# A two-layer trunk in split float32: weight low parts behind the gating, gate's first products ahead of up's, sums between the last transposes, and some pair sums in two DMAs

## The chip, the cores and the metric

The kernel runs on 1 core of one Trainium2 chip. The metric is device time in microseconds of one execution; the time before is the median of 3 runs. Engines are named as the profile names them: PE (matmuls, with PEld for its weight loads), DVE, ACT, POOL and SP; SP issues most DMAs, POOL those that add in flight, ACT a few.

## The reference, cut to what matters

16 learned tokens and 512 given ones make 528 rows of width 1024. Two layers follow, and a last RMSNorm; the learned rows are dropped at the end.

```python
for i in range(DEPTH):                       # 2
    h = h + 0.5 * swiglu(rmsnorm(h, norm_ffn1[i]), ffn1_w_in[i], ffn1_w_out[i])
    h = h + mixer_i(rmsnorm(h, norm_mix[i]))     # retention, then gated linear attention
    h = h + 0.5 * swiglu(rmsnorm(h, norm_ffn2[i]), ffn2_w_in[i], ffn2_w_out[i])
h = rmsnorm(h, final_norm)[:, N_META:]

def swiglu(x, w_in, w_out):
    gate, up = jnp.split(x @ w_in, 2, axis=-1)   # 1024 -> 2 x 2816
    return (jax.nn.silu(gate) * up) @ w_out      # 2816 -> 1024
```

All of it is float32.

## The kernel before, in words

**Layout.** The hidden width lies on the 128 partitions (8 tiles `x[d]`), tokens lie along the free axis, in two halves of 264 columns (256 in the last SwiGLU, which leaves out the learned tokens). The four SwiGLUs are called f10, f20, f11 and f21 (first or second of the layer, then the layer); each has 22 tiles of 128 hidden features for gate and 22 for up.

**Three products for one.** Each float32 operand is split in a high and a low part, `hi` (a cast, L154 for weights, L425 for values, both on ACT) and `lo` (the rest, L155 and L426, on DVE). `mm3` makes one product of three matmuls: hi x hi (L392), hi x lo of the values (L393), lo of the weights x hi (L394).

**Units of seven.** Most weight tiles are used in pairs, by a Strassen-like scheme (`unit_steps`): a unit takes a 2 x 2 block of weights (two feature tiles, two halves of the contraction) and the two token halves, and makes 7 products instead of 8, in the order `a11, s1, s2, a12, s3, s4, a22`. The parts `s1` to `s4` are sums of weight blocks. Two of these sums are made in flight: `pair[:, 0]` and `pair[:, 1]` are loaded with blocks a11 and a22 by SP (L122), and a DMA issued by POOL adds a21 to both (L123). `s1` reads `pair[:, 1]`, `s3` reads `pair[:, 0]`. The other two are made by DVE (L160, L162). Products go to one PSUM bank X and a two-bank tile QZ; ACT copies intermediate results out (L604, L606, L610) before the bank is added to again.

**Weights.** The class `Weights` holds a plan of all weight parts in the order of use. `_load` issues loads as buffers come free (7 raw, 3 pair), `_split` makes a part's `hi` and `lo` (7 buffers). `get` is called at the head of a step, `free` and `hook` (which calls `fetch`, four parts ahead) at its end.

**Order of a SwiGLU** (`ffn_steps`). The first tiles are plain (`"p"`), the others units: gate (`"i", "g"`), then up (`"i", "u"`), then, a gate unit behind the end of a group of hidden tiles, the output units (`"o"`) of that group; f21 has groups of 6, 6, 6 and 4 tiles, the others of 8, 6 and 8. So the output units of f21's first group lie between the gate unit and the up unit of tiles 6 and 7. In the last up unit of f10, f20 and f11 (`last` in `unit_u`) the hidden value is split in two parts: `row1` adds (L830), gates (L831) and calls `hidden(..., 0)`; `c21` gates the rest (L842) and calls `hidden(..., 1)`. The output units of the last group start right behind it.

**Order on the engines.** Each engine runs its instructions in an order that the tile framework lays down when the program is built, by readiness and priority; `urgent()` raises the priority, `issue_after(ins)` puts what is inside behind `ins`. A part that is issued later in the code can therefore stand earlier on an engine.

**Start.** x and the first weights (512 columns each, gate's first) are loaded by SP in turn. Nine matmuls on ones (L356) keep PE busy meanwhile. `plain_first` then makes gate and up of tile 0 together, over 8 contraction tiles k, per k: gate on both halves, then up on both halves, six matmuls each. Meanwhile ACT and DVE scale and split x (L468, L470) and sum its squares (L476 to L487), which PE then reduces (L514).

**End** (`out_last`). The last output tiles are made plainly (`pl`). For the second token half each tile's residual (L976), square (L981 on ACT, summed by DVE at L984) and gained value `xg` (L989) are made as it is finished; the last square is kept apart. Then each `xg[d]` is transposed, 128 tokens at a time (L1033, two per d), PE reduces the squares (L1040), DVE and POOL make the scale (L1045, L1047), ACT and DVE apply it (L1053, L1055), and SP writes four blocks of 128 x 512 (L1056).

Of the kernel before, what the change touches and what calls it, by code (L numbers as in the profile page):

```python
# [13 lines left out]
AF = mybir.ActivationFunctionType  # L14
# [47 lines left out]
class Weights:  # L62
# [10 lines left out]
    def __init__(self, tc, ctx, raw_bufs=7, pair_bufs=3, bufs=7):  # L73
        self.nc, self.tc = tc.nc, tc

        self.behind = None
        self.raw_pool = ctx.enter_context(tc.tile_pool(name="wraw", bufs=raw_bufs))
        self.pair_pool = ctx.enter_context(tc.tile_pool(name="wpair", bufs=pair_bufs))
        self.pool = ctx.enter_context(tc.tile_pool(name="wsplit", bufs=bufs))

        self.homes = [(self.pool, bufs, set())]
        self.ahead = AHEAD


        self.loads = {"raw": [], "pair": []}
        self.begun = dict.fromkeys(self.loads, 0)
        self.over = dict.fromkeys(self.loads, 0)
        self.room = {"raw": raw_bufs, "pair": pair_bufs}
        self.tiles, self.plan, self.parts = {}, [], {}
        self.split = self.taken = self.keys = 0  # L90
# [6 lines left out]
            self.loads["raw"].append(((c, o), len(self.plan), (part,)))  # L97
            self.plan.append((key, c, o, part.shape[1], None))

    def add_unit(self, key, ap1, ap2, order):  # L100
        c = self.keys
        self.keys += 1
        n = ap1.shape[1] // 2
        a = {"a11": ap1[:, :n], "a12": ap1[:, n:], "a21": ap2[:, :n], "a22": ap2[:, n:]}
        self.loads["pair"].append((c, len(self.plan), (a["a11"], a["a22"], a["a21"])))
        for q in ("a11", "a12", "a22"):
            self.loads["raw"].append(((c, q), len(self.plan), (a[q],)))
        for q in order:
            self.plan.append((key + (q,), c, q, n, order))

    def _load(self):
        nc = self.nc
        for kind, loads in self.loads.items():
            while self.begun[kind] < min(self.over[kind] + self.room[kind], len(loads)):
                c, first, aps = loads[self.begun[kind]]
                if kind == "pair" and first > self.split + 3 * len(self.UNIT):
                    break
                n = aps[0].shape[1]
                if kind == "pair":
                    t = self.pair_pool.tile([P, 2, PW], F32, tag="pair", name=f"pair{c}")[:, :, :n]  # L120
                    for i in range(2):
                        nc.sync.dma_start(t[:, i], aps[i])  # L122
                    nc.gpsimd.dma_start(t, aps[2].unsqueeze(1).broadcast_to([P, 2, n]), accum_op=ALU.add)  # L123
                else:
                    t = self.raw_pool.tile([P, PW], F32, tag="raw", name=f"raw{self.begun[kind]}")[:, :n]
                    nc.sync.dma_start(t, aps[0])
                self.begun[kind] += 1
                self.tiles[c] = t

    def _split(self, upto):  # L130
        V = self.nc.vector
        while self.split < min(upto, len(self.plan)):
# [17 lines left out]
            with ExitStack() as order_:  # L150
                if self.behind and i < self.FRONT:
                    for ins in self.behind:
                        order_.enter_context(self.tc.issue_after(ins.ins))
                self.nc.scalar.copy(hi[:, :n], raw)  # L154
                V.tensor_sub(lo[:, :n], raw, hi[:, :n].bitcast(F32))  # L155
            self.parts[i] = (hi, lo)
            self.split += 1
# [55 lines left out]
def trunk(ctx, tc, a):  # L213
# [30 lines left out]
    def plan_ffn(w_in, w_out, layer, which, last=False, late=False):  # L244
        first = True
        for kind, a_, b_ in ffn_steps(last, late):
            key = (which, layer, kind, a_, b_)
            o = b_ + (NF if a_ == "u" else 0)
            if kind == "p":
                if late and b_ == 0:  # L250

                    if a_ == "g":
                        for q in range(2):
                            for s in range(2):
                                W.add((which, layer, kind, "gu"[s], 0, q), w_in[layer, s * NF, :, q * PW:(q + 1) * PW])
                else:
                    W.add(key, w_in[layer, o])
            elif kind == "i":
                W.add_unit(key, w_in[layer, o], w_in[layer, o + 1], W.FIRST if first else W.UNIT)
                first = False  # L260
            else:
                f0, f1 = (LAST_GROUPS if last else GROUPS)[a_]
                c = slice(f0 * P, f1 * P)
                if kind == "o":
                    W.add_unit(key, w_out[layer, b_, :, c], w_out[layer, b_ + 1, :, c], W.UNIT)
                else:
                    W.add(key, w_out[layer, b_, :, c])

# [378 lines left out]
    def ffn(which, layer, halves, gcol, feed, late=False):  # L647
# [5 lines left out]
        with tc.tile_pool(name=f"h_{me}", bufs=4) as hp, tc.tile_pool(name=f"t_{me}", bufs=1) as tp, \  # L653
# [135 lines left out]
            def plain_first():  # L789

                ps, out = zip(*[halves_of(f"p{me}{s}0") for s in "gu"])
                for q in range(2):
                    ws = [W.get((which, layer, "p", s, 0, q)) for s in "gu"]
                    for k in range(KD // 2 * q, KD // 2 * (q + 1)):
                        for i in range(2):
                            for hf, (r0, r1) in enumerate(halves):
                                mm3(ps[i][hf], *W.at(ws[i], k % (KD // 2) * P), uh[k][:, r0:r1], ul[k][:, r0:r1],
                                    k == 0, k == KD - 1)
                    for w in ws:
                        W.free(w)  # L800
                        hook()
# [20 lines left out]
                return g  # L822

            def unit_u(f, g, first):
                y = []
                last = feed and f + 2 == NF

                def row1(ab, qz):
                    o = y[0][:, 2:]
                    V.tensor_add(o, ab, qz)  # L830
                    V.tensor_mul(o, o, pair(g[0], halves))  # L831
                    if last:
                        hidden(f, y[0], 0)

# [6 lines left out]
                def c21(c):  # L841
                    V.scalar_tensor_tensor(y[0][:, 0], c, -1.0, g[1][:, a0:a1], ALU.mult, ALU.mult)  # L842
                    if last:
                        hidden(f, y[0], 1)

                unit((which, layer, "i", "u", f), f"{me}u{f}", W.FIRST if first else W.UNIT, halves, 4, rhs_in, up_,
                     row1, c22, c21)
# [5 lines left out]
            def unit_o(gi, d, behind):  # L853
# [22 lines left out]
                        feed(d + 1, ins)  # L876

                unit((which, layer, "o", gi, d), f"{me}o{gi}{d}", W.UNIT, halves, len(hs), rhs, up_, row1, c22, c21, behind)

            first, outs, g = True, {}, []  # L880
            steps = ffn_steps(feed is None, late)
# [82 lines left out]
    def out_last(key, hh, hl, halves, scale):  # L964
# [67 lines left out]
            for j in range(2):  # L1032
                nc.tensor.transpose(yt[j][:, d // 4, (d % 4) * P:(d % 4 + 1) * P], xg[d][:, j * P:(j + 1) * P], ident)  # L1033

        for d in range(KD - 2):
            turn(d)
        st = bank("st_fb")
        for i, sq in enumerate((sqa[1], last)):
            for j in range(2):
                nc.tensor.matmul(st[:, j:j + 1], lhsT=sq[:, j * P:(j + 1) * P], rhs=ones[:, 0:1],  # L1040
                                 start=(i + j == 0), stop=(i == 1), skip_group_check=True)
        for d in range(KD - 2, KD):
            turn(d)
        ms = tmp.tile([P, 8], F32, tag="ms", name="ms_fb")
        V.tensor_scalar(ms[:, :2], st[:, :2], 1.0 / D, EPS, ALU.mult, ALU.add)  # L1045
        r = tmp.tile([P, 8], F32, tag="r", name="r_fb")
# [1 line left out]
        for b in range(2):  # L1048
            for j in range(2):
                ys = (tmp.tile([P, T], F32, tag="hf", name=f"yb{j}{b}") if j else  # L1050
                      tail_[:, 6 + b, :])[:, :512]
                if j == 0:
                    S.activation(ys, yt[j][:, b, :], AF.Copy, scale=r[:, j:j + 1])  # L1053
                else:
                    V.tensor_scalar(ys, yt[j][:, b, :], r[:, j:j + 1], None, ALU.mult)  # L1055
                nc.sync.dma_start(a["out_b"][j * P:(j + 1) * P, b * 512:(b + 1) * 512], ys)  # L1056


    def retention(feed):
# [974 lines left out]
```

## Time and profile before

| | |
|---|---|
| runs, us | 2075.05, 2076.25, 2075.76; median 2075.76 |
| profiled execution, us | 2076.74, its span 2075.0 |
| mean granted clock of PE | 0.999 |
| DVE, ACT, POOL busy | 86%, 57%, 10% of the span |
| DMA | 318.84 MB, 154 GB/s over the span |

The profile records one execution. A row of the timeline is: start, duration (both us from the span's start), engine, line, operation, output <- inputs, shapes, count, and in brackets the idle time before it with what ended it. A row of windows is: stretch, its length, then busy time and instructions of the engines asked for, the granted clock, the DMA engines' busy share and GB/s. A matmul's duration includes its way through the array; how fast PE works is read from the distance of starts.

### The profile page before, as it was taken

The numbers are of one execution on the slowest core, as the hardware profiler recorded it, in microseconds if no ns is written. First come the engines' busy times: TensorE is split into PE (matmuls) and PEld (weight loads), VectorE is DVE, ScalarE is ACT, GpSimd is POOL, SyncE is SP. The second block draws the span as 40 slices with busy tenths as digits, with TensorE's granted clock in tenths as the row PEclk, the third lists the DMA queues.
The fourth block names the chain that finished last, engine by engine and source line by source line (L and its number), as shares of the span: only waits on it lengthen the run. The fifth ranks groups of instructions, "written<-read, shape, count | busy, mean of one in ns | idle before, by whom it ended". The sixth has DMA issues, their size and how long they took to land. (4 is left out here: it accounts for less than half of the span.)

```text
span 2075.0 us, 42965 instructions
## 1 busy us (share of the span) xinstructions
PE 2062.4 (99%) x16367; PEld 2018.1 (97%) x16367; DVE 1789.7 (86%) x3214; ACT 1192.7 (57%) x2329; POOL 206.1 (10%) x175
## 2 busy tenths in 40 slices
PE   9999999999999999999999999999999999999998
PEld 9999999999999999999999999999999988999998
DVE  8988889968686879988889998889997968998886
ACT  5656566554545455656566565666645445666664
POOL 1011111010101000111111011110101000111110
PEclk9999999999999999999999999999999999999999
DMA  7676777355555532776776377677614351687772
GB/s 223 152 195 158 198 179 188 104 139 137 137 139 126 144 101 69 180 189 159 188 190 183 108 179 182 150 208 174 198 57 122 88 164 61 163 210 174 181 179 72
DMA packets 175871, 318.84 MB, mean 154 GB/s; under 512 B 17456, under 2 KB 40368, under 8 KB 175664
## 3 DMA queue, kind: packets, MB, share of 16 engines
q1 hardware_dynamic: 133856, 237.30, 34.8%
q0 software_dynamic: 40800, 75.51, 23.0%
q10 hardware_dynamic: 1008, 3.29, 0.5%
q8 instruction: 128, 2.10, 0.4%
q14 instruction: 79, 0.65, 0.1%
HBM read 311.76 MB, written 4.26 MB: 152 GB/s over the span
## 5 line engine op out<-in xcount | busy, mean ns | idle before, releaser
L154 ACT CAST whi<-raw 128x512 fp32r<-128x512 f32 (+1 forms) x893 | 526.0, 606 | 484.2 <-DVE raw L160 97.4
L155 DVE TENSOR_TENSOR wlo<-raw,whi 128x512 fp32r<-128x512 f32 (+1 forms) x893 | 584.7, 671 | 145.1 <-ACT whi L154 136.4
L154 ACT CAST whi<-pair 128x512 fp32r<-128x512 f32 (+1 forms) x304 | 183.5, 604 | 120.3 <-PE Xf11u L393 7.3
L155 DVE TENSOR_TENSOR wlo<-pair,whi 128x512 fp32r<-128x512 f32 (+1 forms) x304 | 202.5, 666 | 7.7 <-ACT whi L154 6.3
L123 POOL DMA_DIRECT2D pair<-in_f_in x75 | 91.1, 1214 | 770.5 <-DVE wlo L155 264.1
L160 DVE TENSOR_TENSOR raw<-pair,raw 128x512 f32<-128x512 f32 (+1 forms) x146 | 97.5, 668 | 2.5
L162 DVE TENSOR_TENSOR raw<-raw,raw 128x512 f32<-128x512 f32 (+1 forms) x146 | 97.4, 667 | 2.4
L123 POOL DMA_DIRECT2D pair<-in_f_out x48 | 58.1, 1210 | 413.8 <-DVE wlo L155 161.2
L393 PE MATMUL po_r<-ogl,whi 128*128 128x264 f32 x256 | 72.7, 284 | 0.0
L392 PE MATMUL po_r<-ogh,whi 128*128 128x264 f32 x256 | 72.5, 283 | 0.0
L394 PE MATMUL po_r<-ogh,wlo 128*128 128x264 f32 x256 | 72.5, 283 | 0.0
L123 POOL DMA_DIRECT2D pair<-in_ret_in x20 | 24.3, 1216 | 295.9 <-DMA pair<-in_ret_in 96.8
L392 PE MATMUL Xf20o<-hf,whi 128*128 128x264 f32 x176 | 50.9, 289 | 0.2
L392 PE MATMUL Xf11o<-hf,whi 128*128 128x264 f32 x176 | 50.9, 289 | 0.2
L392 PE MATMUL Xf10o<-hf,whi 128*128 128x264 f32 x176 | 50.8, 289 | 0.2
L393 PE MATMUL Xf10o<-hf,whi 128*128 128x264 f32 x176 | 50.0, 284 | 0.0
L393 PE MATMUL Xf11o<-hf,whi 128*128 128x264 f32 x176 | 50.0, 284 | 0.0
L393 PE MATMUL Xf20o<-hf,whi 128*128 128x264 f32 x176 | 50.0, 284 | 0.0
L394 PE MATMUL Xf11o<-hf,wlo 128*128 128x264 f32 x176 | 49.9, 285 | 0.0
L394 PE MATMUL Xf10o<-hf,wlo 128*128 128x264 f32 x176 | 49.9, 285 | 0.0
L394 PE MATMUL Xf20o<-hf,wlo 128*128 128x264 f32 x176 | 49.9, 284 | 0.0
L394 PEld LDWEIGHTS po_r<-ogh,wlo 128*128 128x128 f32 x256 | 48.2, 188 | 0.0
(985 smaller groups left out, 8519.9 us busy)
## 6 DMA issues: line engine op xcount, KB each, us to landing
raw<-in_f_in SPq DMA_DIRECT2D x277, 256.0 KB, 4.5
pair<-in_f_in SPq DMA_DIRECT2D x150, 256.0 KB, 4.7
pair<-in_f_in POOLq DMA_DIRECT2D x75, 512.0 KB, 6.6
raw<-in_f_out SPq DMA_DIRECT2D x80, 256.0 KB, 3.9
raw<-in_ret_in SPq DMA_DIRECT2D x76, 256.0 KB, 3.4
raw<-in_f_out SPq DMA_DIRECT2D x72, 192.0 KB, 3.2
pair<-in_f_out SPq DMA_DIRECT2D x48, 256.0 KB, 4.2
pair<-in_f_out POOLq DMA_DIRECT2D x24, 512.0 KB, 6.0
```

What stands on the lines that cost most here:

```text
L123: nc.gpsimd.dma_start(t, aps[2].unsqueeze(1).broadcast_to([P, 2, n]), accum_op=ALU.add)
L154: self.nc.scalar.copy(hi[:, :n], raw)
L155: V.tensor_sub(lo[:, :n], raw, hi[:, :n].bitcast(F32))
L160: V.tensor_add(s2, self.tiles[c][:, 1], self.tiles[c, "a11"])
L162: V.tensor_add(raw, raw, s2)
L392: nc.tensor.matmul(ps, lhsT=lh, rhs=rh, start=start, stop=False, **kw)
L393: nc.tensor.matmul(ps, lhsT=lh, rhs=rl, start=False, stop=False, **kw)
L394: return nc.tensor.matmul(ps, lhsT=ll, rhs=rh, start=False, stop=stop, **kw)
```

## The change

Five edits:

1. `Weights.late`: in the last up unit of f10, f20 and f11 the gating's multiplication (L831) is kept; from the end of `c21` to the end of the next output unit every low part of a weight (L155) is issued behind it.
2. `plain_first`: for k = 0, up's six products are issued behind gate's last.
3. `parted`: for the two input units of tiles 6 and 7 of f21 and the four output units of its first group, SP loads `pair[:, 1]` first, and POOL adds a21 in two DMAs, `pair[:, 1]` first, instead of one.
4. The end: the sums of squares come behind the transposes of 4 tiles instead of 6; the other 4 tiles are issued behind them.
5. The output: the first block is scaled and written in two halves of 256 columns, and the last block is written by a DMA that ACT issues.

```diff
-                    for i in range(2):
+                    for i in (1, 0) if parted[0] else (0, 1):
                         nc.sync.dma_start(t[:, i], aps[i])
-                    nc.gpsimd.dma_start(t, aps[2].unsqueeze(1).broadcast_to([P, 2, n]), accum_op=ALU.add)
+                    if parted[0]:
+                        for i in (1, 0):
+                            nc.gpsimd.dma_start(t[:, i], aps[2], accum_op=ALU.add)
+                    else:
+                        nc.gpsimd.dma_start(t, aps[2].unsqueeze(1).broadcast_to([P, 2, n]), accum_op=ALU.add)
...
                 self.nc.scalar.copy(hi[:, :n], raw)
+                if self.late:
+                    order_.enter_context(self.tc.issue_after(self.late.ins))
                 V.tensor_sub(lo[:, :n], raw, hi[:, :n].bitcast(F32))
...
-                W.add_unit(key, w_in[layer, o], w_in[layer, o + 1], W.FIRST if first else W.UNIT)
+                W.add_unit(key, w_in[layer, o], w_in[layer, o + 1], W.FIRST if first else W.UNIT,
+                           last and b_ == LAST_GROUPS[1][0])
...
-                    W.add_unit(key, w_out[layer, b_, :, c], w_out[layer, b_ + 1, :, c], W.UNIT)
+                    W.add_unit(key, w_out[layer, b_, :, c], w_out[layer, b_ + 1, :, c], W.UNIT, last and a_ == 0)
...
-                            for hf, (r0, r1) in enumerate(halves):
-                                mm3(ps[i][hf], *W.at(ws[i], k % (KD // 2) * P), uh[k][:, r0:r1], ul[k][:, r0:r1],
-                                    k == 0, k == KD - 1)
+                            with tc.issue_after(ins.ins) if k == 0 and i == 1 else ExitStack():
+                                for hf, (r0, r1) in enumerate(halves):
+                                    ins = mm3(ps[i][hf], *W.at(ws[i], k % (KD // 2) * P), uh[k][:, r0:r1],
+                                              ul[k][:, r0:r1], k == 0, k == KD - 1)
...
-                    V.tensor_mul(o, o, pair(g[0], halves))
+                    late[0] = V.tensor_mul(o, o, pair(g[0], halves))
...
                     if last:
                         hidden(f, y[0], 1)
+                        W.late = late[0]
...
                 unit((which, layer, "o", gi, d), f"{me}o{gi}{d}", W.UNIT, halves, len(hs), rhs, up_, row1, c22, c21, behind)
+                W.late = None
...
-        for d in range(KD - 2):
+        for d in range(KD - 4):
             turn(d)
...
-        for d in range(KD - 2, KD):
-            turn(d)
+        with tc.issue_after(ins.ins):
+            for d in range(KD - 4, KD):
+                turn(d)
...
-                nc.sync.dma_start(a["out_b"][j * P:(j + 1) * P, b * 512:(b + 1) * 512], ys)
+                for o in (0, 256) if b + j == 0 else (0,):
+                    c = slice(o, 256 + o if b + j == 0 else 512)
+                    if j == 0:
+                        S.activation(ys[:, c], yt[j][:, b, c], AF.Copy, scale=r[:, j:j + 1])
+                    else:
+                        V.tensor_scalar(ys[:, c], yt[j][:, b, c], r[:, j:j + 1], None, ALU.mult)
+                    (nc.scalar if b + j == 2 else nc.sync).dma_start(
+                        a["out_b"][j * P:(j + 1) * P, b * 512 + c.start:b * 512 + c.stop], ys[:, c])
```

`ins` in the end is the last of the matmuls that reduce the squares.

More of the change, by code (lines that the diff above doesn't have):

```diff
@@ L76, in __init__ @@
         self.behind = None
+        self.late = None
         self.raw_pool = ctx.enter_context(tc.tile_pool(name="wraw", bufs=raw_bufs))
@@ L98, in add, with add_unit @@
             self.plan.append((key, c, o, part.shape[1], None))
-    def add_unit(self, key, ap1, ap2, order):
+    def add_unit(self, key, ap1, ap2, order, parted=False):
         c = self.keys
@@ L104, in add_unit @@
         a = {"a11": ap1[:, :n], "a12": ap1[:, n:], "a21": ap2[:, :n], "a22": ap2[:, n:]}
-        self.loads["pair"].append((c, len(self.plan), (a["a11"], a["a22"], a["a21"])))
+        self.loads["pair"].append((c, len(self.plan), (a["a11"], a["a22"], a["a21"]), parted))
         for q in ("a11", "a12", "a22"):
@@ L114, in _load @@
             while self.begun[kind] < min(self.over[kind] + self.room[kind], len(loads)):
-                c, first, aps = loads[self.begun[kind]]
+                c, first, aps, *parted = loads[self.begun[kind]]
                 if kind == "pair" and first > self.split + 3 * len(self.UNIT):
@@ L824, in unit_u @@
             def unit_u(f, g, first):
-                y = []
+                y, late = [], [None]
                 last = feed and f + 2 == NF
@@ L1039, in out_last @@
             for j in range(2):
-                nc.tensor.matmul(st[:, j:j + 1], lhsT=sq[:, j * P:(j + 1) * P], rhs=ones[:, 0:1],
-                                 start=(i + j == 0), stop=(i == 1), skip_group_check=True)
-        for d in range(KD - 2, KD):
-            turn(d)
+                ins = nc.tensor.matmul(st[:, j:j + 1], lhsT=sq[:, j * P:(j + 1) * P], rhs=ones[:, 0:1],
+                                       start=(i + j == 0), stop=(i == 1), skip_group_check=True)
+        with tc.issue_after(ins.ins):
+            for d in range(KD - 4, KD):
+                turn(d)
         ms = tmp.tile([P, 8], F32, tag="ms", name="ms_fb")
@@ L1051, in out_last @@
                       tail_[:, 6 + b, :])[:, :512]
[L1052 to L1055, printed above, removed]
-                nc.sync.dma_start(a["out_b"][j * P:(j + 1) * P, b * 512:(b + 1) * 512], ys)
+                for o in (0, 256) if b + j == 0 else (0,):
[6 more added lines that the diff above has]
+                        a["out_b"][j * P:(j + 1) * P, b * 512 + c.start:b * 512 + c.stop], ys[:, c])
     def retention(feed):
```

## The prediction

> **What bounds the kernel now.** I read the page first, then the waits of PE, then stretches of the timeline around each of them.
>
> ```profile
> span 2075.0 us, 42965 instructions
> ...
> PE 2062.4 (99%) x16367; PEld 2018.1 (97%) x16367; DVE 1789.7 (86%) x3214; ACT 1192.7 (57%) x2329; POOL 206.1 (10%) x175
> ...
> PE pf10u L392 <- ACT whi L154: 1.0, 1, 1.0
> PE QZf21o L392 <- ACT suf21o L604: 0.9, 1, 0.9
> ```
>
> PE has work in 2062.4 of 2075.0 us, and the change takes no product away. What can be won is what PE loses between products, and the tail behind the last one. The waits of PE that stand as idle time are few, and these two, the longest after the start-up, lie where the change edits. But busy time is modelled and hides short waits, so I also counted products in equal stretches. The last three columns of the next rows don't matter here; x is the number of instructions that lie in the stretch.
>
> ```profile
> 314.59:318.50 3.91, 3.70 (x29) 1.00 1.00 321
> ...
> 1434.66:1438.57 3.91, 3.70 (x29) 1.00 0.95 308
> 1100.74:1104.65 3.91, 3.91 (x35) 1.00 0.71 210
> ```
>
> The first two are the beginnings of the last output group of f10 and f11, right behind their last up unit; f20, the third place of this kind, lies between them with the same count in its 3.91 us from 1088.02. The last row is a settled stretch of f20's group. Six products fewer in the same time: with 32 starts in 3.91 us a product takes 0.122 us, so each of the three places loses 6 x 0.122 = 0.73 us, of which only 3.91 - 3.70 = 0.21 us shows as idle.
>
> **Low parts behind the gating (three places).**
>
> ```profile
> 1087.65 0.69 DVE L155 TENSOR_TENSOR wlo<-raw,whi 128x512 fp32r<-128x512 f32 x1
> 1088.25 0.70 DVE L831 TENSOR_TENSOR yf<-yf,gf 128x528 f32<-128x528 f32 x1
> ...
> 1086.67 0.62 ACT L154 CAST whi<-raw 128x512 fp32r<-128x512 f32 x1 [0.83 <-PE QZf20u L393]
> 1088.15 0.62 ACT L154 CAST whi<-raw 128x512 fp32r<-128x512 f32 x1 [0.86 <-PE Xf20u L393]
> 1088.99 0.98 ACT L425 CAST hf<-yf 128x264 fp32r<-128x264 f32 x2 [0.22 <-DVE yf L831]
> ...
> 1089.11 0.28 PE L392 MATMUL QZf20o<-hf,whi 128*128 128x264 f32 x1
> 1089.46 0.39 PE L392 MATMUL Xf20o<-hf,whi 128*128 128x264 f32 x1
> 1089.68 0.29 PE L393 MATMUL QZf20o<-hf,whi 128*128 128x264 f32 x1
> ...
> 1090.90 0.28 PE L392 MATMUL QZf20o<-hf,whi 128*128 128x264 f32 x1
> 1091.34 0.39 PE L392 MATMUL Xf20o<-hf,whi 128*128 128x264 f32 x1
> ...
> 1090.66 0.62 ACT L154 CAST whi<-raw 128x512 fp32r<-128x512 f32 x1 [0.38 <-ACT hf L425]
> ```
>
> Between the sum of the last up unit (L830) and its gating (L831) a weight's low part slips in and holds the gating by 0.60 us (1088.25 - 1087.65). The cast of the hidden value waits for the gating, and the product at 1089.46 for that cast: its gap is 1089.46 - 1089.11 - 0.12 = 0.23 us, and the product behind it comes 0.22 us later instead of 0.12, 0.33 us in all. The second gap, up to 1091.34, ends with a cast of later weights (1090.66 + 0.62 = 1091.28); it takes the rest, 0.40. Does the edit reach this low part? The cast of its weight began when PE had finished a step of the up unit and set a buffer free; there are seven buffers, so it belongs to a part seven places on, in the output unit, and that is issued after `W.late` has been set. So I take it that it does.
>
> With the gating 0.60 us earlier the cast is held by ACT alone, which is in L154 up to 1088.77 (1088.15 + 0.62); the product followed its cast's start by 0.47 (1089.46 - 1088.99), so it could run at 1089.24, and its turn is at 1089.23. The first gap goes. What is late next is the second gap, which hangs on PE's own progress through the weight buffer and moves along with it. The moved low part has to run somewhere: right behind L831 it delays the rest of the hidden value as before (then the place gives as little as 0), later it gives up to the whole 0.73; its own consumer is several steps of 12 products (1.46 us each) away, which covers it. I take the first gap alone: 3 x 0.33 = **1.0 us**, bounds 0 and 3 x 0.73 = 2.2.
>
> **Pair sums in two DMAs.**
>
> ```profile
> 1816.01 1.20 POOL L123 DMA_DIRECT2D pair<-in_f_in  x1 [7.33 <-DVE raw L162]
> ...
> DMA to landing us min/median/max: 5.3/6.9/9.5
> ...
> 1824.21 0.62 ACT L154 CAST whi<-raw 128x512 fp32r<-128x512 f32 x1
> 1825.65 0.62 ACT L154 CAST whi<-pair 128x512 fp32r<-128x512 f32 x1 [0.82 <-DMA raw<-in_f_in]
> 1826.18 0.37 ACT L604 COPY suf21o<-QZf21o 128x256 f32<-128x256 f32 x1
> ...
> 1825.42 0.28 PE L394 MATMUL Xf21o<-hf,wlo 128*128 128x256 f32 x1
> ...
> 1826.59 0.39 PE L392 MATMUL QZf21o<-hf,whi 128*128 128x256 f32 x1 [0.89 <-ACT suf21o L604]
> ```
>
> (The second row is of the pair sums between 1800 and 1827 us, four of them, 384 and 512 KB.) The cast of up unit 6's first sum stands in ACT's queue ahead of the copy L604, and PE waits for that copy. The cast waits for its pair sum: issued at 1816.01, landed after the longest time of the four, 9.5 us, so at 1825.5. ACT names a raw load, but the cast reads `pair`. With the half that is read first in a DMA of its own, and its plain load first on SP's queue, 256 KB have to land instead of 512. No row shows such a DMA: the bounds are 9.5 us (halving brings nothing) and 5.3 us, the quickest row; I take 5.3, as the size is below any in the rows. It lands by 1821.3, 3 us early. Then the cast follows its predecessor, starts by 1824.21 + 0.53 = 1824.74 (0.53 is the step from 1825.65 to 1826.18), and the copy and PE come 1825.65 - 1824.74 = 0.9 us earlier. Bounds: 0, and the whole gap, 1826.59 - 1825.42 - 0.12 = 1.05. I take **0.9 us**. The price is six more issues of 1.20 us on POOL, which is busy 10% and had been idle for 7.33 us here; if the second halves came late, the steps that read them lie two products' steps (over 2 us) behind the first.
>
> The Trainium skill ("DMA: Bandwidth & Descriptors", section on the anatomy of a SWDGE DMA) speaks against splitting: each such DMA has about 2.0 us fixed and the rest goes by bytes at 436 GB/s, so 256 KB less would be worth only 0.6 us. By that estimate this term would be about 0.6 us instead of 0.9; the rows above, 5.3 to 9.5 us, lie far over its 3.2 us for 512 KB.
>
> **Gate's six products first.**
>
> ```profile
> 5.39 0.69 DVE L155 TENSOR_TENSOR wlo<-raw,whi 128x512 fp32r<-128x512 f32 x1
> ...
> 6.92 0.39 PE L392 MATMUL pf10u<-uha,whi 128*128 128x264 f32 x1 [1.01 <-ACT whi L154]
> ...
> 7.27 0.28 PE L394 MATMUL pf10g<-uha,wlo 128*128 128x264 f32 x1
> ...
> 7.63 0.28 PE L394 MATMUL pf10g<-uha,wlo 128*128 128x264 f32 x1
> ...
> 4.54:7.96 3.42, 2.18 (x12) 1.40 (x12) 2.33 (x4) 2.29 (x5) 0.00 (x0) 1.00 0.97 308
> 7.96:11.37 3.41, 3.41 (x17) 3.41 (x17) 3.14 (x5) 3.41 (x7) 0.00 (x0) 0.50 1.05 405
> ...
> 2066.19:2069.61 3.42, 2.25 (x22) 2.01 (x20) 1.14 (x4) 1.55 (x4) 0.69 (x1) 1.00 0.00 0
> ...
> 18.34 0.71 DVE L487 TENSOR_TENSOR sqa_n<-sqa_n,sq_n 128x528 f32<-128x528 f32 x1
> ...
> 20.03 1.17 PE L514 MATMUL st_n<-ones,sqa_n 128*128 128x1 f32 x10
> ```
>
> Up's first product waits until 6.92 with four of gate's behind it (7.27 to 7.63), whose last operand was there at 5.39 + 0.69 = 6.08. They move into the wait: 4 x 0.12 = **0.48 us**. The order that is added costs nothing here: gate's last operand is there 0.84 us before up can start. There is more at stake: after the stretch up to 7.96, in which PE was busy 2.18 us, the granted clock is 0.50 for 3.41 us. In the stretch at the end with 2.25 us busy it stayed 1.00. Four products more make 2.66, so the clock may hold. But PE then meets the sums of squares (L514), which need L487, done at 19.05: more than 20.03 - 19.05 = 0.98 us can't be won, with whatever clock. And in an execution in which the clock does not fall anyway, PE already stands there and wins 0. Bounds 0 and 0.98; I take the middle, the products alone.
>
> The Trainium skill ("TensorE: Matmul & The Clock Gate", part 1) has the clock halved only after a whole idle window of about 3.4 us, with windows that run free of the kernel; by that nothing would be at stake here. The rows disagree on the first (halved after 2.18 us of work); the second no row here can show. By the skill this term would still be 0.48.
>
> **The end.**
>
> ```profile
> 2065.89 1.31 PE yt L1033 x12
> 2067.20 0.34 PE st_fb L1040 x4
> 2067.54 0.17 PE yt L1033
> ...
> 2068.37 0.73 POOLq L2029
> ...
> 2066.45 0.42 ACT L981 ACTIVATE sqf<-x 128x256 f32<-128x256 f32 x1
> ...
> 2069.12 1.27 ACT L1053 ACTIVATE endl<-yt,r_fb 128x512 f32<-128x512 f32 x2 [1.86 <-POOL r_fb L1047]
> ```
>
> In the chain the sums of squares stand behind 13 transposes; now 8. Five fewer: 4 x 0.109 (1.31 / 12) + 0.17 = 0.61 us. The last square is there at 2066.87 and the sums of it would begin at 2066.76 + 0.34 = 2067.10, so nothing holds them. The eight transposes left, 0.9 us, run beside the scale and POOL's 0.73. Then the first output piece is half as wide on ACT (256 columns took 0.42 in L981, 512 here 1.27 / 2 = 0.64), so its DMA starts some 0.2 us sooner, and a fifth issue is added (one is moved to ACT's queue, behind ACT's last work); the four 256 KB outputs follow one another closely, so between -0.2 and +0.3 I take 0.1. Together **0.7 us**, bounds 0.4 and 0.9.
>
> **Sum.** 1.0 + 0.9 + 0.48 + 0.7 = 3.1 us. The profiled execution took 2076.74 us, 1.74 us more than its span, and should come to 2073.7. The median of the runs lies 0.98 below it: 2075.76 - 3.1 = **2072.7 us**, 0.15% faster, less than the 0.2% that a measurement of this kernel can tell from no change.
>
> **Rivals.**
> - *More than the first gap.* The low part runs behind the whole hidden value, all three places close (2.2) and the clock holds (0.98): 2.2 + 0.9 + 0.98 + 0.7 = 4.8 us, 2071.0. For it: DVE works without a break there, so 0.60 us less ahead of the chain could move all of it. Against: the second gap hangs on ACT and PE. 18%.
> - *The waits are only moved, or the first edit doesn't do what it says.* The low part was issued before `W.late` is set, or lands right behind L831 (0); PE meets the squares at 19.05 as before (0); pair sum and end stay: 0.9 + 0.7 = 1.6 us, 2074.2. 24%.
> - *Slower: products put ahead of their operands.* PE's order is laid down when the program is built, and from the first edit on it is laid down anew. The product at 1091.34 waits for weights of a later unit that had just been cast; such a one costs 0.32 + 0.10 = 0.42 us (1091.34 - 1090.90 - 0.12, and a slow successor). Eight new ones (3.1 / 0.42) would eat the gain; with 18 the kernel takes 2075.76 - 3.1 + 18 x 0.42 = 2080.2, over 0.2% slower. Against: three such places in 2075 us. 4%.
> - The forecast, 1.6 to 4.1 us gained: 54%.
>
> **Numbers.** Lower bounds of all terms: 0 + 0 + 0 + 0.4; upper: 2.2 + 1.05 + 0.98 + 0.9 = 5.1, so 2070.6. The runs shown lie 1.2 us apart; the upper end takes in the moved waits and ends at 2075.2. Faster by over 0.2% (below 2071.6) needs most of the first rival: 0.18. Slower by over 0.2% is the third: 0.03. Within: 0.79.
>
> **What would show it.** Right: L831 directly behind L830 at the three places and about 29 to 32 products in their 3.91 us (x32 to x35 by the row's count); no wait QZf21o for L604; gate's six products done before 6.9 us, st_n near 19.5 or, with a full clock, 19.05; eight transposes ahead of the sums and POOL's power 0.6 us sooner after the last product. Wrong: a new wait among PE's longest, a place with fewer than 26 starts, or a gain at the start that is gone by the next wait for squares or loads.

## The result: slower by 0.17%, and the profile after

| | us | against before |
|---|---|---|
| before, 16 runs | 2075.33 (2074.15 to 2076.42) | |
| after, 16 runs beside them | 2078.85 (2077.41 to 2082.07) | 1.0017, 95% interval 1.0010 to 1.0025 |
| after, 11 runs of a second series | 2078.54 (2076.73 to 2080.43) | 1.0015, 1.0006 to 1.0024 |
| profiled execution of after | 2078.70, span 2076.9 | |

The kernel is slower by some 3.4 us (3.5 in the first series, 3.3 in the second); 3.1 us faster was predicted. The head of the page of after, and then its longest waits of PE (total, times, longest):

```profile
span 2076.9 us, 42971 instructions
...
PE 2063.5 (99%) x16367; PEld 2018.2 (97%) x16367; DVE 1790.0 (86%) x3214; ACT 1192.7 (57%) x2330; POOL 209.2 (10%) x181
```

```profile
PE st_n L524 <- DVE sqa_n L495: 1.3, 1, 1.3
...
PE Xrg L402 <- DVE vl L555: 0.7, 1, 0.7
PE Xf20o L402 <- ACT suf20o L616: 0.6, 1, 0.6
PE Xf11o L402 <- ACT suf11o L616: 0.6, 1, 0.6
PE Xf10o L402 <- ACT suf10o L616: 0.6, 1, 0.6
```

The wait QZf21o for a copy is gone, and that of pf10u. New are three waits of 0.6 us at the three places of the first edit, one of 0.7 for a product of retention (Xrg), and one of 1.3 us for the sums of squares at the entry to gated linear attention (GLA), some 45 us behind the third place, in code that the diff doesn't touch.

**At a place.** After, DVE, ACT and PE at f20 (start, duration, engine, line, shapes, count, and in brackets what was waited for). Line numbers differ from kernel to kernel: L843 here is L831 of before, L164 is L155.

```profile
1087.17 0.70 DVE L842 TENSOR_TENSOR yf<-suf20u,QZf20u 128x528 f32<-128x528 f32 x1
1087.91 0.71 DVE L843 TENSOR_TENSOR yf<-yf,gf 128x528 f32<-128x528 f32 x1
1088.54 0.69 DVE L164 TENSOR_TENSOR wlo<-pair,whi 128x512 fp32r<-128x512 f32 x1
...
1090.58 0.42 DVE L854 SCALAR_TENSOR_TENSOR yf<-Xf20u,gf 128x264 f32<-128x264 f32 x1
...
1093.81 1.28 DVE L164 TENSOR_TENSOR wlo<-raw,whi 128x512 fp32r<-128x512 f32 x2
...
1089.56 0.39 PE L402 MATMUL Xf20o<-hf,whi 128*128 128x264 f32 x1
...
1092.61 0.39 PE L402 MATMUL Xf20o<-hf,whi 128*128 128x264 f32 x1 [0.61 <-ACT suf20o L616]
...
1091.34 0.63 ACT L435 CAST hf<-yf 128x528 fp32r<-128x528 f32 x1
1091.87 0.41 ACT L435 CAST hf<-ttf20h 128x264 fp32r<-128x264 f32 x1
1092.18 0.37 ACT L616 COPY suf20o<-Xf20o 128x264 f32<-128x264 f32 x1
```

The gating L843 follows the addition L842 directly, as the edit says, and the first gap ends at 1089.56 instead of 1089.46 in a kernel that here runs 0.42 us late: it closed by 0.32 us, as predicted. But the edit reaches three low parts, not one. The one from `pair` lands directly behind the gating, the rest of the gating (L854) comes at 1090.58, and the casts that hang on it stand on ACT ahead of the copy L616, for which PE now waits 0.61 us. The two from `raw` run only at 1093.81.

**At an entry.** The held low part is the last reader of its buffer, so the load that waits for this buffer goes later. At f20 the low part that slipped in ended at 1087.65 + 0.69 = 1088.34 in before, and SP issued a raw load right behind it; in after the low parts from `raw` run at 1093.81 and the load goes at 1094.56:

```profile
1088.37 5.03 SPq L126 DMA_DIRECT2D raw<-in_f_out  x2
```

```profile
1094.56 0.93 SPq L133 DMA_DIRECT2D raw<-in_f_out  x2
```

The loads behind it stand in another order on SP's queue. Before, then after, ahead of GLA: POOL's pair sum, the cast on ACT that stands ahead of the scaling of x, and the sums of squares on PE; and, of after, the stretch behind (length, busy PE and instructions, granted clock, DMA share, GB/s):

```profile
1461.19 1.21 POOL L123 DMA_DIRECT2D pair<-in_gla_in  x1 [7.53 <-DVE wlo L155]
...
1475.83 0.62 ACT L154 CAST whi<-raw 128x512 fp32r<-128x512 f32 x1 [1.11 <-DMA raw<-in_gla_in]
...
1480.22 1.25 PE L514 MATMUL st_n<-ones,sqa_n 128*128 128x1 f32 x10
```

```profile
1467.66 1.21 POOL L130 DMA_DIRECT2D pair<-in_gla_in  x1 [14.72 <-DVE wlo L164]
...
1476.27 0.62 ACT L161 CAST whi<-raw 128x512 fp32r<-128x512 f32 x1 [2.27 <-DMA raw<-in_gla_in]
...
1477.89 0.62 ACT L161 CAST whi<-raw 128x512 fp32r<-128x512 f32 x1 [0.80 <-DMA raw<-in_gla_in]
...
1478.61 0.73 ACT L478 ACTIVATE uha<-x,gains 128x528 fp32r<-128x528 f32 x1
...
1482.59 1.25 PE L524 MATMUL st_n<-ones,sqa_n 128*128 128x1 f32 x10 [1.26 <-DVE sqa_n L495]
```

```profile
1483.74:1487.15 3.41, 3.41 (x12) 0.50 1.08 229
```

After runs 0.84 us late here. The pair sum goes 6.47 us later (1467.66 - 1461.19), 5.63 without that delay, so its transfer falls into the raw loads of the entry: the two ahead of the scaling take 6.0 and 4.8 us from issue to landing instead of 2.8 and 3.8. The last cast ahead of the scaling (L478) waits for its load until 1477.89 instead of 1475.83, x is scaled, squared and summed later, PE waits 1.26 us for the sums, and then the granted clock is 0.50 for 3.41 us.

### The profile page after: what moved, and what is told of

The parts are those of the page before. It is cut to its first block, busy times and chain, and to the rows that moved or that the text cites. A ratio compares the mean times of both kernels' runs of the same rounds, so it can differ in the third digit from the quotient of the medians.

```text
span 2076.9 us, 42971 instructions
## 1 busy us (share of the span) xinstructions
PE 2063.5 (99%) x16367; PEld 2018.2 (97%) x16367; DVE 1790.0 (86%) x3214; ACT 1192.7 (57%) x2330; POOL 209.2 (10%) x181
## 5 line engine op out<-in xcount | busy, mean ns | idle before, releaser
L164 DVE TENSOR_TENSOR wlo<-raw,whi 128x512 fp32r<-128x512 f32 (+1 forms) x893 | 582.3, 668 | 143.8 <-ACT whi L161 136.5
L164 DVE TENSOR_TENSOR wlo<-pair,whi 128x512 fp32r<-128x512 f32 (+1 forms) x304 | 201.6, 663 | 7.0 <-ACT whi L161 5.4
L130 POOL DMA_DIRECT2D pair<-in_f_out x44 | 53.2, 1208 | 386.6 <-DVE wlo L164 113.5
```

## The experiments

Each profile is compared with that of before through the start of the same product, by its number in PE's order; the table below gives by how much the difference grows over a stretch. The stretches are, in us of before: places 314 to 322, 1085 to 1092, 1433 to 1441; entries 345 to 489 (retention), 1125 to 1157 (f11), 1472 to 1491 (GLA).

**The first edit alone, and all but it**

```diff
# e1_late_only: before, and of the change only this
+                if self.late:
+                    order_.enter_context(self.tc.issue_after(self.late.ins))
                 V.tensor_sub(lo[:, :n], raw, hi[:, :n].bitcast(F32))
# e2_no_late: after, without this
```

> The first edit alone on the kernel before. Loads theory (the held low parts are the last readers of raw weight buffers, so the loads that wait for these buffers go later; this costs little at the three places and more at the entries to the mixers): slower than before by 4 to 5.5 us, about 2080; the matmul that reduces the squares at the entry to the second mixer (GLA) waits again more than 1 us for the sums of squares, and the raw load that followed at 1088.37 comes some 6 us later. Planning theory (the order laid down anew for edits 2 to 5 costs, not the first edit): within 1 us of before. Site theory (the loss is at the three places themselves, since the rest of the gating and the copies of products come later there): slower by 1 to 2 us, with the loss inside the 6 us behind each of the three places and nothing at GLA's entry.

> All edits but the first. Loads theory and site theory: the other edits bring what the comparison of the two traces shows up to the places of the first edit and behind them, about 1.0 us at the start, 1.2 at the pair sum and 0.6 at the end: 2.5 to 3 us faster than before, about 2072.5, and no wait of over 1 us at GLA's entry. Planning theory: 2075 or more, with the wait at GLA's entry still there.

Measured: the first edit alone 2078.36 against 2074.88, ratio 1.0019 (1.0010 to 1.0027); the others together 2074.74, ratio 0.9997 (0.9988 to 1.0006), which is -0.14 us, between -2.5 and +1.2. So the whole loss is the first edit's, by 3.5 us (the loads theory had said 4 to 5.5), and the planning theory in its first form (the other edits' new order costs) falls. But the second expectation missed too: the 2.5 to 3 us that the two profiles seemed to show for the other edits aren't there in the medians.

**The other edits one at a time**

```diff
# e7_gate_only: before, with edit 2
+                            with tc.issue_after(ins.ins) if k == 0 and i == 1 else ExitStack():
# e8_parted_only: before, with edit 3
+                        for i in (1, 0):
+                            nc.gpsimd.dma_start(t[:, i], aps[2], accum_op=ALU.add)
# e12_end_only: before, with edits 4 and 5
-        for d in range(KD - 2):
+        for d in range(KD - 4):
```

> The second edit alone. Prediction: 0.48 us faster, up to 0.98. Chance theory (the half clock from 7.96 on belongs to the one profiled execution of before, since the runs without this edit kept the full clock there as well): within 0.3 us of before in the median, full clock at the start, st_n at about 18.5 to 19.5 us; and the wait of QZf21o for a copy at 1826.59 is there or not by chance as well.

> The third edit alone. Prediction: 0.9 us faster. Chance theory (the wait of 0.9 us before QZf21o belongs to the profiled execution: three runs without this edit did not have it): within 0.4 us of before in the median, and no half clock at the start although gate and up come in the order of before.

> The fourth and fifth edits alone. Prediction: 0.7 us faster (0.4 to 0.9). The profile of the kernel without the first edit gave 0.26 us from the first transpose to the span's end; by that it is 0.2 to 0.4 us faster, because part of the 0.61 us that the sums come earlier is not on the path behind them.

Measured: 2075.41 against 2075.22 (1.0001, 0.9992 to 1.0010), 2074.68 against 2075.22 (0.9997, 0.9988 to 1.0006), 2075.14 against 2075.45 (0.9997, 0.9989 to 1.0006): none can be told from no change. Where the two larger gains went is shown best by the run e5 (below), whose instructions stand in the order of before on every engine. Its start, and then e5 where before waited 0.89 us for a copy:

```profile
7.96:11.37 3.41, 3.41 (x21) 1.00 1.04 398
```

```profile
10.19 0.42 PE L401 MATMUL pf10g<-ula,whi 128*128 128x264 f32 x1
10.41 0.36 PE L402 MATMUL pf10g<-uha,wlo 128*128 128x264 f32 x1
10.60 0.28 PE L401 MATMUL pf10u<-ula,whi 128*128 128x264 f32 x1
10.72 0.28 PE L402 MATMUL pf10u<-uha,wlo 128*128 128x264 f32 x1
```

```profile
1814.80 1.20 POOL L130 DMA_DIRECT2D pair<-in_f_in  x1 [6.50 <-DVE x L871]
...
1824.49 0.62 ACT L162 CAST whi<-pair 128x512 fp32r<-128x512 f32 x1
1825.01 0.37 ACT L612 COPY suf21o<-QZf21o 128x256 f32<-128x256 f32 x1
...
1825.16 0.28 PE L402 MATMUL Xf21o<-hf,wlo 128*128 128x256 f32 x1
1825.43 0.39 PE L400 MATMUL QZf21o<-hf,whi 128*128 128x256 f32 x1
```

*The start.* The clock column of e5 says 1.00, but the trace has no record of the clock before 10.55 us, and up to there products start 0.22 us apart (10.41 - 10.19), behind it 0.12. So e5, too, starts at half speed, and its sums of squares (st_n) start at 19.97, where before's start at 20.03. In the 14 other profiles, ten of them without the second edit, st_n starts at 18.40 to 19.09, and always 0.05 or 0.06 us behind the end of the last square. In these PE stands waiting for the squares, whatever the order of gate and up, and there is nothing for the edit to win. Half speed as late as in before and e5 is in two of the twelve profiles without the edit and in none of the four with it; whether the edit makes it rarer isn't shown, and the median gained nothing.

*The pair sum.* PE reaches QZf21o 0.27 us after its predecessor without parted sums. In the profiles of all 14 runs of this study, eleven of them without the third edit, the stretch from 1815 to 1827 is 0.93 or 0.94 us shorter than in the profile of before. So that wait belonged to the one profiled execution of before, which lies 1.86 us over the median of 2074.88. Its sum landed after 9.5 us; in e5 it was issued 1.2 us earlier, landed after 7.1, at 1821.87, and was in time.

The end does gain. Alone (e12):

```profile
2063.77 1.04 PE L1033 MATMUL yt<-ident,endh 128*128 128x128 f32 x8
2064.78 0.60 PE L1040 MATMUL st_fb<-ones,endl 128*128 128x1 f32 x4
2065.25 0.58 PE L1040 MATMUL st_fb<-ones,sqf 128*128 128x1 f32 x4
...
2065.87 0.16 DVE L1046 TENSOR_SCALAR ms_fb<-st_fb 128x2 f32<-128x2 f32 x1 [1.14 <-PE st_fb L1040]
```

and before:

```profile
2065.73 1.47 PE L1033 MATMUL yt<-ident,endh 128*128 128x128 f32 x12
2067.04 0.50 PE L1040 MATMUL st_fb<-ones,endl 128*128 128x1 f32 x4
...
2068.09 0.16 DVE L1045 TENSOR_SCALAR ms_fb<-st_fb 128x2 f32<-128x2 f32 x1 [1.41 <-PE st_fb L1040]
```

From the first transpose to the mean square it takes 2.10 us instead of 2.36, and from there to the end of the span nothing is won (6.85 to 6.91 us in the four profiles with these edits, 6.87 to 6.90 in the twelve without): from the first transpose to the end it is 8.95 to 9.01 us in those four and 9.23 to 9.27 in the others, so some 0.27 us less. The first sum starts 1.01 us behind the first transpose (2064.78 - 2063.77) instead of 1.31: 0.30 and not 4 x 0.109, as DVE's last sum is there only at 2064.73 (L984, 2064.32 + 0.41). From the first sum to the mean square it takes 1.09 us instead of 1.05: the transpose that stood between the sums is gone from there, but the eight sums in a row take as long.

**Which low parts, and where**

```diff
# e3_late_next: before, with edit 1 and the held low parts ahead of other work
                 if self.late:
                     order_.enter_context(self.tc.issue_after(self.late.ins))
+                    order_.enter_context(self.tc.high_priority(offset=4 * HEAD_START))
# e4_second_next: the same, for the second part of each place alone
+                if self.late and self.held == 2:
```

> The first edit alone, but the three held low parts of each place run directly behind the gating of the second half instead of several instructions later. Loads theory: the raw buffers come free some 2 to 5 us earlier than with the first edit, the loads keep their order, GLA's entry loses its wait, and the time is within 1.5 us of before. Site theory: the three low parts (3 x 0.69 us) stand ahead of the rest of the hidden value at each place, which makes the places worse: 3 x 0.7 to 3 x 2 us slower than before, however the loads go.

> The first edit cut to the one low part that the prediction saw between the addition and the gating (one of three at each place), which runs directly behind the gating; the other two stay where they were before. Loads theory: one raw buffer is freed 0.7 us later and nothing else moves: within 1 us of before, no wait at GLA's entry. Site theory: the first gap (0.33 us) closes at each place if DVE's rest does not come later, so 0 to 1 us faster. If it is slower by over 2 us, both are wrong and it is the moved gating itself.

Measured: 2078.92 against 2074.88, 1.0021 (1.0012 to 1.0030), and 2084.99, 1.0045 (1.0032 to 1.0057). What was lost where, in us (negative: won):

| profile | place f10 | retention | place f20 | f11 | place f11 | GLA | half clock from |
|---|---|---|---|---|---|---|---|
| after | 0.45 | 0.85 | 0.25 | 0.10 | 0.18 | 3.01 | 1483.74 |
| after, second series (e14) | 0.45 | 1.35 | 0.26 | 0.79 | 0.19 | 1.37 | - |
| first edit alone (e1) | 0.46 | 2.73 | 0.26 | 0.16 | 0.18 | 1.27 | 361.55 |
| all but the first edit (e2) | -0.02 | 0.02 | -0.01 | 0.20 | -0.01 | 0.19 | - |
| three parts next (e3) | 0.76 | 1.32 | 0.58 | 0.27 | 0.78 | 0.17 | - |
| one part next (e4) | -0.24 | 2.39 | -0.25 | 3.52 | -0.22 | 2.31 | 1136.74 |
| e4, pairs together (e6) | -0.23 | 1.94 | -0.25 | 4.80 | -0.32 | 4.65 | 1135.16 and 1486.73, twice 3.41 |
| e4, raw loads first (e11) | -0.24 | 1.79 | -0.25 | 2.08 | -0.32 | 5.40 | 1135.80; 1483.96, twice 3.41 |
| before, one load held (e9) | -0.02 | -0.14 | -0.01 | 0.02 | -0.02 | 0.82 | - |
| before, SP exchanged (e10) | -0.03 | 0.75 | -0.01 | 0.95 | -0.01 | 0.54 | - |
| before, pair behind raw (e13) | 0.00 | 0.00 | -0.01 | 0.26 | -0.02 | 1.63 | - |
| order of before (e5) | -0.01 | 0.01 | 0.00 | 0.20 | -0.01 | 0.02 | - |

Each single edit (e7, e8, e12) lost up to 0.39 at retention, 0.30 at f11 and 0.54 at GLA in its one profile; the two profiles of the same kernel after differ by 0.50, 0.69 and 1.64 there (the last with a half clock in one of them). So a number of this size at an entry needs its rows beside it.

One reading holds for all rows at f11 and GLA: what is lost there is how much later the sums of squares start than in before (st_n), and 1.7 us more for each 3.41 us at half clock, within 0.5 us in every one of the 15 profiles. At retention it isn't enough: in the eight profiles without the first edit it holds within 0.2 us, in the seven with it, in whatever form, 0.15 to 1.6 us more are lost, the wait of Xrg among them.

With three parts next (e3) the loads keep their order (but for one exchange, near 1188) and GLA loses next to nothing, as the loads theory said; the places lose 2.1 us, as the site theory said; with the entries that makes 3.9, more than the loads theory allowed. With the one part that the prediction had seen (e4), each place wins 0.22 to 0.25 us: the predicted 0.33 in mechanism. But 10.1 us are lost in the median. Its profile, of an execution 3.5 us below that median, shows them at the entries: 8.2 us. So neither theory stands as I had put it: the places win what they should (0.71 us), and over ten times as much is lost at the entries behind them.

**SP's queue**

In e4, ahead of f11's entry: SP's order and the cast that stands ahead of the scaling on ACT; then the same rows of before:

```profile
1125.42 0.80 SPq L123 DMA_DIRECT2D pair<-in_f_in  x2
1126.60 1.53 SPq L127 DMA_DIRECT2D raw<-in_f_in  x3
...
1131.60 0.62 ACT L155 CAST whi<-raw 128x512 fp32r<-128x512 f32 x1 [2.56 <-DMA raw<-in_f_in]
1132.13 0.73 ACT L474 ACTIVATE uha<-x,gains 128x528 fp32r<-128x528 f32 x1
```

```profile
1124.77 0.33 SPq L122 DMA_DIRECT2D pair<-in_f_in  x1
1125.33 0.33 SPq L126 DMA_DIRECT2D raw<-in_f_in  x1
1125.71 0.42 SPq L122 DMA_DIRECT2D pair<-in_f_in  x1
...
1129.33 0.62 ACT L154 CAST whi<-raw 128x512 fp32r<-128x512 f32 x1 [1.47 <-DVE wlo L155]
1129.92 0.74 ACT L468 ACTIVATE uha<-x,gains 128x528 fp32r<-128x528 f32 x1
```

In before the raw load goes between the halves of a pair, at 1125.33, and its cast ends as x becomes ready: the scaling starts at 1129.92. In e4 the load goes behind both halves, at 1126.60, the cast waits 2.56 us for it, and the scaling behind it on ACT starts at 1132.13, 1.93 us late beyond the 0.28 that e4 is behind here. Six runs test this.

```diff
# e5_loads_late: before, one raw load at each place behind a product
+                    with self.tc.issue_after(self.hold.ins) if held else ExitStack():
                         nc.sync.dma_start(t, aps[0])
# e9_loads_hold: the same with a real wait, by a copy on POOL
+                    if held:
+                        nc.gpsimd.tensor_copy(t[:, :1], self.hold)
# e10_swap_only: before, pairs 50 and 129 ahead of one raw load
+                    with self.tc.high_priority(offset=HEAD_START) if c in EARLY else ExitStack():
# e13_pairs_late: before, pairs 49, 128 and 173 behind raw loads
+                        with self.tc.issue_after(self.raws[BEHIND[c] + i].ins) if c in BEHIND else ExitStack():
# e6_second_next_sp: e4, the halves of nine pairs together and earlier
+                    with self.tc.high_priority(offset=3 * HEAD_START) if c in EARLY else ExitStack():
# e11_second_next_raw: e4, the second half of three pairs behind a raw load, six pairs earlier
+                            with self.tc.issue_after(self.first[c].ins) if i and c in BEHIND else ExitStack():
```

> The kernel before with one raw load at each of the three places held until the last product of the first output unit of the last group; the order on every engine is that of before, low parts and gating too. In the kernel before the load at the second place is issued at 1088.37; it should now go at about 1094.5, as late as in the run with the first edit alone (1096.67, less its 2.7 us of lead). Loads theory: the three places keep their times, the loads behind go later too, and the entries behind the places cost: 1.5 to 4 us slower than before. Planning theory (what costs is the order of ACT, DVE and PE that is laid down anew, in all variants with the first edit): within 0.7 us of before.

> The kernel before with one raw load at each of the three places held for real: a copy of one column by POOL into its buffer waits for the second output tile of the first output unit. ACT, DVE and PE have the order of before, SP issues the held load one place later. Loads theory: the load goes at about 1095 instead of 1088.37, the ones behind it follow later, and the entries behind the places cost 1 to 4 us; the places themselves keep their times. Planning theory (the loss comes with the new order on ACT, DVE and PE): within 0.7 us of before.

> The kernel before with one exchange on SP's queue ahead of two entries (retention and f11): the second half of a pair goes ahead of one raw load instead of behind it, as in the two slowest runs; nothing else moves. Loads theory in its sharp form (the raw load at each entry whose cast stands on ACT ahead of the scaling of x sets the entry): 1 to 3 us slower, at those two entries only, with GLA's entry as before. Planning theory: within 0.4 us of before.

> The kernel before; only SP's queue differs: at each of the three places the two halves of one pair go behind one and behind three more raw loads (with the first edit they go behind one and behind two). ACT, DVE and PE keep the order of before. Loads theory: POOL's sum of that pair goes about 5 us later (1466 instead of 1461.19 ahead of GLA) and shares the DMA engines with the raw loads of the entry (1470.47 and 1471.98), which land 1 to 2 us later; GLA's entry loses 0.7 to 3 us, depending on the clock; 1 to 3 us slower than before. Planning theory: within 0.5 us of before.

> As the run with one low part directly behind the gating (10.1 us slower than before, entries 7.9 us worse in its profile), but SP issues both halves of a pair together ahead of the raw loads, as in the kernel before; ACT, DVE and PE keep that run's order. Loads theory: the pair sums land earlier, the casts at the entries no longer wait on ACT ahead of the scaling of x, and most of the 7.9 us goes: 0 to 3 us slower than before. Planning theory: as slow as that run, 8 to 10 us over before.

> As the run with one low part directly behind the gating (entries 7.9 us worse), but the second half of the pair at each entry goes behind that raw load, as in before, and behind some more raw loads; ACT, DVE and PE keep that run's order. Loads theory in its sharp form: f11's entry loses less than 1 us instead of 3.5, and the total is 0 to 3 us over before. Planning theory: 7 to 10 us over before.

- e5: 2075.42 against 2075.22, 1.0000 (0.9991 to 1.0009). It tests nothing of the loads: the load still went at 1087.97, since the constraint changed no order and added no wait. It serves as a second profile of before's order.
- e9: 2075.47 against 2075.45, 0.9999 (0.9990 to 1.0008), though the load went at 1099.74 instead of 1088.37. One late load at the place costs nothing in the median; against the loads theory in its first form.
- e10: 2076.80 against 2075.45, 1.0004 (0.9995 to 1.0013). The median can't tell. In the profile the two entries with the exchange lose 0.75 and 0.95, and the rows at f11 say why: the cast waits 2.52 us for its load, and the scaling behind it starts 0.98 us later than in before.
- e13: 2077.35 against 2075.23, 1.0009 (1.0001 to 1.0018): slower by 2.1 us, with nothing moved on ACT, DVE, PE and POOL. It shows the entry of after again:

```profile
1465.64 1.21 POOL L128 DMA_DIRECT2D pair<-in_gla_in  x1 [12.99 <-DVE x L868]
...
1476.56 0.62 ACT L159 CAST whi<-raw 128x512 fp32r<-128x512 f32 x1 [1.67 <-DMA raw<-in_gla_in]
...
1480.88 1.25 PE L519 MATMUL st_n<-ones,sqa_n 128*128 128x1 f32 x10 [1.45 <-DVE sqa_n L490]
```

The run is 0.94 us ahead here, so the pair sum goes 5.4 us later than in before (1465.64 + 0.94 - 1461.19), the cast starts 1.67 later (1476.56 + 0.94 - 1475.83), and st_n waits 1.45 us. The two raw loads of the entry take 4.7 and 5.4 us to land instead of 2.8 and 3.8. The place of pair loads on SP's queue is enough to make the wait of GLA's entry. The same exchange ahead of retention and f11 cost nothing or little (0.00 and 0.26).

- e6 and e11: 2082.48 against 2075.22 (1.0038, 1.0025 to 1.0051) and 2080.21 against 2075.45 (1.0024, 1.0015 to 1.0033). Pairs moved together (e6) didn't help; with the raw loads ahead (e11) f11's entry lost 2.08 us instead of 3.52, more than the 1 us that I had set, and the total, 4.8 us over before, lies between the two theories. At GLA both lost more than e4, and there the clock was halved twice.

**The kernel after once more** (unchanged)

> The kernel after, unchanged, for a second profile. If the losses belong to the kernel: the copies L616 are waited for 0.6 us at all three places again, Xrg waits for L555 0.7 us, and st_n of GLA waits over 0.7 us, with or without a half clock; about 3.5 us slower than before in the median. If the wait of st_n belonged to that one execution: no wait over 0.5 us there, and the span 2 to 3 us shorter than 2076.9.

The waits came back: L616 0.6 us three times, Xrg 0.7, st_n 1.2, this time without a half clock. They belong to the kernel; the half clock is there or not.

No run was faster than the kernel before by more than its interval.

## Why the prediction was wrong

- **Low parts behind the gating (+1.0 us predicted, -3.5 measured): the step that failed.** "The moved low part has to run somewhere [...] its own consumer is several steps [...] away, which covers it." I asked who reads the low part, and not whose buffer it frees: it is the last reader of a raw or pair buffer, and so sets when SP's next loads can go (1094.56 instead of 1088.37 at f20); the loads behind were queued in another order, too. This returns as far as 45 us later, at entries where x becomes ready just as the last cast ends (1129.92 and 1129.33 + 0.62 at f11 in before), so that nothing may come later. The gap itself was rightly read: 0.32 closed at f20, and 0.22 to 0.25 net in e4. And the edit reaches three low parts, where the prediction saw one; with three the places lose 0.18 to 0.45 each instead of winning.
- **Pair sums (0.9):** the size of the landing was right: 256 KB land in 5.1 us (median, e8), close to the 5.3 taken. What failed is that the wait was taken for the kernel's; it stood in one execution of before only, and the median gained 0.54 us, not apart from no change.
- **Gate's six (0.48):** the step that failed is to price the products. The text said that it wins 0 "in an execution in which the clock does not fall anyway", as PE meets the squares; this is the common case (14 of 16 profiles), and it still took 0.48. The median lost 0.19, not apart from no change.
- **The end (0.7):** right in kind, some 0.27 in size, below the bound of 0.4. The failed step is "nothing holds them": DVE's sum holds them (2064.73), so the four transposes gave 0.30 instead of 0.44; the fifth gave nothing instead of 0.17, as the sums in a row take 1.09 us to the mean square instead of 1.05; and the two halves and the moved issue of the output gave nothing instead of 0.1.
- **The slower rival** had products ahead of their operands as its mechanism. Of that kind only the copies L616 and Xrg came, about 1.4 us together (0.45 + 0.25 + 0.18 + 0.48, the last the loss at Xrg in both profiles of after, a part of retention's). The larger part, the late loads and the waits at the entries, was no rival at all.
- The Trainium skill ("DMA: Bandwidth & Descriptors", anatomy of a SWDGE DMA) makes the halving of such a DMA worth 0.6 us. Beside the other loads of this stretch the sums of 512 KB took 7.1 to 9.7 us (before, e5 and e8) and those of 256 KB 5.0 and 5.3 (e8), so at least 1.7 us less. The median gained nothing from it, as the sum is in time without it.

**Open.** At f11 and GLA late loads are enough to make losses of this size, though in after ACT's order ahead of these entries differs, too. Loads alone, with the order of before on ACT, DVE and PE, cost 1.63 at GLA (e13) and 0.95 at f11 (e10), and in e11 the scaling at f11 starts 0.5 us late instead of 1.9 (e4), which with 1.7 us for a half clock of 3.41 makes 2.2, close to the 2.08 that were lost. At retention loads alone cost 0.75 (e10), but every kernel with a form of the first edit loses more than its late squares explain, e3 1.32 us with the loads of before's order. This points to the new order on ACT, DVE and PE for a part of it; no run shows that order without the first edit, and how the loss divides isn't settled.

## What to carry to other kernels

When an instruction is moved, list the buffers that it is the last to read, and follow each to the load that waits for it, to what stands behind that load on its queue, and to the first place where a late load meets work that has no slack, even if that is tens of us away. Before a wait is priced as a gain, make sure that it is in more than one execution: here the profile that showed the wait of 0.9 us lay 1.9 us above the median, which was the hint.

## What the runs showed of the hardware

The granted clock halves after windows that are far from idle, and the busy time of the profile alone doesn't decide it: PE was busy 2.15 us of the 3.41 ahead of the half clock in after, 2.47 in e4, 3.02 in e1, and 1.96 in a stretch of that length around the wait of e13, where it stayed at 1.00. The windows of e4, the one ahead and the halved one:

```profile
1133.33:1136.74 3.41, 2.47 (x18) 1.00 0.99 197
1136.74:1140.15 3.41, 3.41 (x17) 0.50 0.51 160
```

The Trainium skill ("TensorE: Matmul & The Clock Gate", part 1) has it halve only after a whole idle window; the rows disagree. A wait of 1.2 to 1.5 us at an entry thus costs itself, and sometimes 1.7 us more. The half clock shows in the spread of the runs (4.7 us for after, 2.3 for before): of the 16 runs of after the two longest, 2080.75 and 2082.07 us, have a mean granted clock of 0.997, the five shortest 0.999 or 1.000. Whether it is all of the spread isn't shown.

The clock column says 1.00 also where the trace has no record of the clock. At the start of e5 it does so up to 10.55 us, with products 0.22 us apart, which is nearly twice the 0.12 behind it; the distance of starts is the surer sign.
